# The next head's queries and keys placed before the second half of a head's attention blocks

## The chip, the cores and the metric

The kernel runs on one core of a Trainium2 chip. The metric is device time of one execution in microseconds (us), as the median of several runs. TensorE (PE) multiplies matrices, VectorE (DVE), ScalarE (ACT) and GpSimd (POOL) work element by element, and SyncE (SP) starts most transfers. Each engine takes its instructions strictly in the order in which the program lists them for it, and waits where an operand or a buffer isn't ready.

## The reference

Two residual layers with a pre-RMSNorm each, over 16 meta tokens and 1024 tokens of width 1024: a gated convolution layer, then a differential-attention layer with 8 heads, and a final RMSNorm. The change concerns the attention layer, which computes, in outline,

```
q, k, v, z = split(hn @ w_in)                       # per head: two q and two k of width 64, v of width 128
for i in range(9):                                  # blocks of 128 queries
    s = q_block @ k[:end].T * scale - slope * distance, masked
    p = softmax(s)
    a = p[first] - lam * p[second]
    o_block = a @ v[:end]
o = rms_norm(o, subln_gain) * (1 - lambda_init) * silu(z)
return o @ w_out
```

## The kernel before

Matrices are multiplied in float32r. A product with a weight is made of three passes (high part of the weight by high and by low part of the input, low part of the weight by the high part), so that one projected strip of 128 channels costs 24 matmuls per chunk of tokens. The input of the attention layer stays in SBUF for the whole layer.

For each head four things are made. `queries(h)` (L903) projects two chunks of 512 tokens into two PSUM banks of the pool "proj", which has two banks in all; DVE takes each chunk out with a scale (L910) into a tile "qt" of the pool "ev", which has two tiles; ACT and POOL split it (L915, and L157 through the helper). `keys(h)` (L921) does the same with three chunks of 348, 346 and 346 tokens (L925, L928, L157) and then copies the half tiles across partitions with four transfers on SP's queue (L934). `gate(h)` (L937) projects two chunks of 512, takes them into two "zt" tiles of the same pool "ev" (L944), and ACT makes their SiLU (L946), with a table load before and one behind it (L946, L948). The SiLU's result is the tile "za", of which there is one: it can't be written before the head before has read its own for the last time (L1055, in the last of its four block pairs). `attention(h, ...)` (L965) has four rounds j = 0 to 3, each of two blocks of 128 queries. Per block and per half m it makes scores in chunks of at most 512 columns (two matmuls each, L989 and L990) in a pool of three PSUM banks. DVE reduces them out of PSUM (L992), ACT exponentiates (L997), ACT and DVE normalise and combine (L1012, L1013), PE transposes (L1023, and L1034 for the last 16 columns), ACT and DVE take the transposes out in two parts (L1027, L1028). At the end of a round PE multiplies with the values (L207 into o, closed by the matmul of L1050), DVE multiplies with the gate (L1055), PE sums squares (L1063), ACT, POOL and DVE normalise, and SP stores the round to memory (ya_d, L1084). In the last head's time PE also begins the output projection (ao), for which SP reloads the stored rounds (L1132).

Nobody writes the engines' order by hand. The program is written head after head, and a scheduler with a timeline of its own picks, at each step, among the instructions that it takes for ready the one that stands first in the program; so the program's order is a priority. In the names of tiles, `s4_3_1_264` is head 4, block 3, half 1, first column 264; `q5_1` is head 5, chunk 1; `o3_3` is head 3, round 3; `tp` and `tc` are transposes. The call that the change rewrites is

```
ops = q2, *keys(0)
for h in range(HEADS):
    attention(h, *ops, sz)
    if h + 1 < HEADS:
        ops = queries(h + 1), *keys(h + 1)
        sz = gate(h + 1)
```

so that a head's queries, keys and gate stand behind the whole of the head before, and fill PE wherever attention isn't ready.

Of the kernel before, what the change touches and what calls it, by code (L numbers as in the profile page):

```python
# [28 lines left out]
HEADS = 8  # L29
# [66 lines left out]
def trunk(  # L96
# [25 lines left out]
    def stage(n, name, dt=F32):  # L122
        return gp.tile([P, T], dt, tag=f"st{n % 2}", name=name, bufs=1)

    def proj(name):
        return psg.tile([P, 512], F32, tag="proj", name=name, bufs=2)
# [29 lines left out]
    def lo_part(eng, out_, full, hi):  # L156
        return eng.tensor_tensor(out=out_, in0=full, in1=hi, op=ALU.subtract)  # L157
# [87 lines left out]
    def project(w, hh, hl, bank, chunks, release=False):  # L245

        wh, wl = w
        if release:
            os = [bank(ci) for ci in range(len(chunks))]
            for k in range(KD):  # L250
                for o, (c0, n) in zip(os, chunks):
                    cs = slice(c0, c0 + n)
                    passes(
                        o[:, :n], [wh[:, k]], [wl[:, k]], [hh[k][:, cs]], [hl[k][:, cs]],
                        start=k == 0, stop=k == KD - 1,
                    )
            for o, (c0, n) in zip(os, chunks):
                yield c0, n, o[:, :n]
            return
        for ci, (c0, n) in enumerate(chunks):  # L260
            o = bank(ci)
            passes(
                o[:, :n],
                [wh[:, k] for k in range(KD)],
                [wl[:, k] for k in range(KD)],
                [hh[k][:, c0 : c0 + n] for k in range(KD)],
                [hl[k][:, c0 : c0 + n] for k in range(KD)],
            )
            yield c0, n, o[:, :n]
# [473 lines left out]
    with ExitStack() as st1:  # L743
# [4 lines left out]
        def qk(name, shape=(P, T), dt=F32R):  # L748
            return sb.tile(list(shape), dt, tag="qk", name=name, bufs=12)
# [4 lines left out]
        def ev(name):  # L754
            return sb.tile([P, 512], F32, tag="ev", name=name, bufs=2)
# [148 lines left out]
        def queries(h):  # L904
            qs = -(2.0 ** (h + 1)) / math.sqrt(HD)
            q2 = [qk(f"q{m}_{h}", (P, SEQ)) for m in range(2)]
            for c0, w, o in project(weights.get(), hh, hl, lambda ci: proj(f"q{h}_{ci}"), RQ):
                cs = slice(c0 - META, c0 - META + w)
                t = ev(f"qt{h}_{c0}")[:, :w]
                V.scalar_tensor_tensor(  # L910
                    out=t, in0=o, scalar=qs, in1=rst[:, c0 : c0 + w], op0=ALU.mult, op1=ALU.mult
                )
                for m in range(2):
                    ms, other = slice(64 * m, 64 * m + 64), slice(64 - 64 * m, 128 - 64 * m)
                    A.activation(out=q2[m][ms, cs], in_=t[ms], func=AF.Copy)  # L915
                    lo_part(G, q2[m][other, cs], t[ms], q2[m][ms, cs].bitcast(F32))
            return q2

        def keys(h):
            k2 = [qk(f"k{m}_{h}") for m in range(2)]  # L920
            kl2 = [qk(f"kl{m}_{h}") for m in range(2)]  # L921
            for c0, w, o in project(weights.get(), hh, hl, lambda ci: proj(f"k{h}_{ci}"), CH):
                cs = slice(c0, c0 + w)
                t = ev(f"kt{h}_{c0}")[:, :w]
                V.tensor_tensor(out=t, in0=o, in1=rst[:, cs], op=ALU.mult)  # L925
                for m in range(2):
                    ms = slice(64 * m, 64 * m + 64)
                    A.activation(out=k2[m][ms, cs], in_=t[ms], func=AF.Copy)  # L928
                    lo_part(V if KL == "V" else G, kl2[m][ms, cs], t[ms], k2[m][ms, cs].bitcast(F32))

            for m in range(2):
                ms, other = slice(64 * m, 64 * m + 64), slice(64 - 64 * m, 128 - 64 * m)
                for t in (k2[m], kl2[m]):
                    SP.dma_start(out=t[other].bitcast(F32), in_=t[ms].bitcast(F32))  # L934
            return k2, kl2

        def gate(h):  # L937
            s = stage(1, f"za{h}")
            for c0, w, o in project(weights.get(), hh, hl, lambda ci: proj(f"za{h}_{ci}"), RQ, h in GREL):
                t = ev(f"zt{h}_{c0}")  # L940
                if h == 0:
                    A.activation(out=t, in_=o, func=AF.Copy)
                    o = t
                V.tensor_tensor(out=t, in0=o, in1=rst[:, c0 : c0 + w], op=ALU.mult)  # L944
                with tc.issue_after(last_exp) if h == 0 else ExitStack():
                    silu = A.activation(out=s[:, c0 - META : c0 - META + w], in_=t, func=AF.Silu).ins  # L946
            with tc.issue_after(silu):
                A.preload_act_table_set("natural_log_exp_and_others")  # L948
            return s
# [14 lines left out]
        def attention(h, q2, k2, kl2, sz):  # L964
# [6 lines left out]
            for j in range(4):  # L971
# [111 lines left out]
                if h < HEADS - 1:  # L1083
                    SP.dma_start(out=ya_d[h, :, :, js], in_=y2.bitcast(F32))  # L1084
                elif j > 1:
                    y_last.append([yh, yl])

        sz = gate(0)
        wv = [value_weights(0)]
# [3 lines left out]
            values(half, *wv[half])  # L1093
        ops = q2, *keys(0)
        for h in range(HEADS):
            attention(h, *ops, sz)
            if h + 1 < HEADS:
                ops = queries(h + 1), *keys(h + 1)
                sz = gate(h + 1)


        def strip_pair(make):
# [176 lines left out]
def _program(arrays):  # L1279
    import concourse.bacc as bacc  # L1280

    nc = bacc.Bacc("TRN2", target_bir_lowering=False, num_devices=1, dynamic_dma_scratch_size=8192)
    args = [
        nc.dram_tensor(n, a.shape, mybir.dt.from_np(a.dtype), kind="ExternalInput").ap() for n, a in arrays.items()
    ]
    args.append(nc.dram_tensor("out", (KD, P, SEQ), F32, kind="ExternalOutput").ap())
    with tile.TileContext(nc, schedule_with_timeline_sim=TLS) as tc:
        trunk(tc, *args)
    return nc
# [9 lines left out]
```

## Time and profile before

| | |
|---|---|
| time, median of 3 runs | 1468.54 us (1467.7 to 1470.9) |
| the profiled execution | 1467.64 us |
| its span, first to last instruction | 1465.5 us |
| mean granted TensorE clock | 0.991 of full speed |
| PE busy | 1423.4 us, 97% |
| DVE, ACT, POOL busy | 1115.3, 887.3, 811.7 us |

A busy PE includes the modelled tail of each matmul, so that a row of one instruction is longer than the distance to the next one. "x12" joins twelve instructions in sequence. Square brackets at the end of a row give the engine's idle time ahead of it, and what ended that. SPq is SP's queue.

### The profile page before, as it was taken

The numbers are of one execution on the slowest core, as the hardware profiler recorded it, in microseconds if no ns is written. First come the engines' busy times: TensorE is split into PE (matmuls) and PEld (weight loads), VectorE is DVE, ScalarE is ACT, GpSimd is POOL, SyncE is SP. The second block draws the span as 40 slices with busy tenths as digits, with TensorE's granted clock in tenths as the row PEclk, the third lists the DMA queues.
The fourth block names the chain that finished last, engine by engine and source line by source line (L and its number), as shares of the span: only waits on it lengthen the run. The fifth ranks groups of instructions, "written<-read, shape, count | busy, mean of one in ns | idle before, by whom it ended". The sixth has DMA issues, their size and how long they took to land.

```text
span 1465.5 us, 24123 instructions
## 1 busy us (share of the span) xinstructions
PE 1423.4 (97%) x8828; PEld 1333.3 (91%) x8828; DVE 1115.3 (76%) x2100; ACT 887.3 (61%) x1615; POOL 811.7 (55%) x646
## 2 busy tenths in 40 slices
PE   8999999999999999999999999999999999999997
PEld 7999999999999999899999878988889899897786
DVE  7989899899899988979545311578788787786774
ACT  7565665565555658766324411568778777786652
POOL 4598999999999940035014500525345354353572
PEclk9999999999999999999999999999999999999998
DMA  5021112112211333554443634223221322338532
GB/s 182 30 73 44 58 52 66 44 44 67 64 44 44 102 108 95 190 166 147 165 167 124 204 99 125 59 73 106 84 81 62 114 80 77 109 88 296 166 121 95
DMA packets 79928, 150.82 MB, mean 103 GB/s; under 512 B 6977, under 2 KB 46402, under 8 KB 78786
## 3 DMA queue, kind: packets, MB, share of 16 engines
q1 hardware_dynamic: 66706, 126.69, 27.3%
q0 software_dynamic: 3824, 13.37, 2.8%
q10 hardware_dynamic: 9280, 9.23, 2.0%
q8 instruction: 69, 1.13, 0.3%
q14 instruction: 49, 0.40, 0.1%
HBM read 106.73 MB, written 34.01 MB: 96 GB/s over the span
## 4 chain that ended last, share of the span: by engine, by line
PE 47%; POOL 18%; DVE 14%; ACT 8%; issue 8%; DMA 4%; SPq 1%; POOLq 0%; DVEq 0%; ACTq 0%
POOL pb L511 16%; PE c L207 8%; PE v L207 6%; PE k L207 5%; PE q L207 4%; PE za L207 4%; PE ao L207 3%; PE o L207 3%; PE u L207 3%; PE z L207 2%; DVE wl L157 2%; PE s L989 2%; ACT pr L510 2%; PE s L990 2%; PE tp L1023 2%
## 5 line engine op out<-in xcount | busy, mean ns | idle before, releaser
L511 POOL TENSOR_TENSOR pb<-pr,pb 128x521 f32<-128x521 f32 (+1 forms) x272 | 389.2, 1440 | 24.9 <-ACT pr L510 10.4
L510 ACT ACTIVATE pr<-vr,chn 128x521 f32<-128x521 f32 x224 | 150.6, 725 | 122.5 <-POOL pb L511 122.1
L207 PE MATMUL c<-b,wh 128*128 128x260 f32 x1024 | 187.3, 285 | 3.0 <-DVE b L157 1.9
L524 DVE SCALAR_TENSOR_TENSOR ev<-vr,chn,ev 128x520 f32<-128x520 f32 x240 | 181.2, 755 | 1.2
L189 ACT ACTIVATE wh<-wf 128x1024 fp32r<-128x1024 f32 x115 | 121.0, 1053 | 99.6 <-PE c L207 54.0
L207 PEld LDWEIGHTS c<-b,wh 128*128 128x128 f32 x1024 | 159.7, 191 | 3.8 <-DVE b L157 2.1
L207 PE MATMUL g<-hp,wh 128*128 128x346 f32 (+1 forms) x752 | 151.8, 329 | 7.6 <-ACT hp L383 3.6
L207 PE MATMUL u<-hp,wh 128*128 128x346 f32 (+1 forms) x752 | 155.9, 321 | 2.0 <-ACT wh L189 2.0
L207 PE MATMUL c<-b,wl 128*128 128x260 f32 x512 | 145.4, 286 | 3.8 <-DVE wl L157 3.8
L157 DVE TENSOR_TENSOR wl<-wf,wh 128x1024 fp32r<-128x1024 f32 x81 | 118.4, 1463 | 30.3 <-ACT wh L189 29.5
L157 POOL TENSOR_TENSOR wl<-wf,wh 128x1024 fp32r<-128x1024 f32 x34 | 85.7, 2521 | 92.9 <-ACT wh L189 47.4
L207 PEld LDWEIGHTS g<-hp,wh 128*128 128x128 f32 x752 | 127.6, 193 | 9.5 <-ACT hp L383 3.9
L207 PE MATMUL z<-hp,wh 128*128 128x346 f32 (+1 forms) x768 | 135.6, 321 | 0.5 <-ACT sig L469 0.5
L524 DVE SCALAR_TENSOR_TENSOR od<-xs,wc,od 128x520 f32<-128x520 f32 x176 | 132.6, 754 | 0.0
L696 POOL TENSOR_TENSOR total<-hsq,total 128x520 f32<-128x520 f32 x12 | 20.6, 1714 | 196.2 <-ACT hsq L695 196.2
L207 PEld LDWEIGHTS u<-hp,wh 128*128 128x128 f32 x752 | 125.7, 188 | 2.8 <-ACT wh L189 2.8
L207 PEld LDWEIGHTS z<-hp,wh 128*128 128x128 f32 x768 | 124.3, 188 | 0.9 <-ACT sig L469 0.7
L997 ACT ACTIVATE p<-p,st 128x272 f32<-128x272 f32 (+7 forms) x128 | 100.5, 785 | 39.3 <-DVE st L992 38.8
L207 PEld LDWEIGHTS c<-b,wl 128*128 128x128 f32 x512 | 97.7, 191 | 4.6 <-DVE wl L157 4.4
L207 PE MATMUL g<-hp,wl 128*128 128x346 f32 (+1 forms) x376 | 84.2, 322 | 0.0
L207 PE MATMUL v<-wv,g 128*128 128x512 f32 x352 | 83.5, 394 | 0.0
L989 PE MATMUL s<-k,q 128*128 128x256 f32 (+6 forms) x224 | 77.2, 349 | 5.3 <-DVE st L992 5.3
(292 smaller groups left out, 3465.1 us busy)
## 6 DMA issues: line engine op xcount, KB each, us to landing
wf<-conv_in SPq DMA_DIRECT2D x48, 512.0 KB, 3.5
wf<-conv_out SPq DMA_DIRECT2D x32, 512.0 KB, 4.1
wf<-attn_in SPq DMA_DIRECT2D x32, 512.0 KB, 3.8
wf<-attn_out SPq DMA_DIRECT2D x17, 512.0 KB, 3.7
sz_d<-sz ACTq DMA_DIRECT2D x32, 260.0 KB, 4.4
szr<-sz_d SPq DMA_DIRECT2D x16, 520.0 KB, 4.4
v<-v_d POOLq DMA_DIRECT2D x8, 1024.0 KB, 5.3
ya_d<-yb SPq DMA_DIRECT2D x28, 256.0 KB, 2.5
```

Source lines behind the costliest of these rows:

```text
L157: return eng.tensor_tensor(out=out_, in0=full, in1=hi, op=ALU.subtract)
L189: A.activation(out=wh, in_=wf, func=AF.Copy)
L207: PE.matmul(o, a[k], b[k], start=start and i == 0, stop=stop and i == tot - 1)
L510: A.activation(out=d, in_=src, func=AF.Copy, scale=w)
L511: G.tensor_tensor(out=dst, in0=d, in1=dst, op=ALU.add)
L524: V.scalar_tensor_tensor(out=dst, in0=src, scalar=w, in1=dst, op0=ALU.mult, op1=ALU.add)
L696: (V if SQA[m] == "V" else G).tensor_tensor(out=total[:, ns], in0=sq, in1=total[:, ns], op=ALU.add)
L989: PE.matmul(o[:, :wm], q2[m][:, qs], k2[m][:, c0 : c0 + wm], start=True, stop=False)
L990: PE.matmul(o[:, :wm], q2[m][:, qs], kl2[m][:, c0 : c0 + wm], start=False, stop=True)
L997: A.activation(out=p[:, :n], in_=p[:, :n], func=AF.Exp, scale=-1.0, bias=least, accum_out=st[:, 1:2],)
L1023: PE.transpose(tp[:, (kb - kb0) * P : (kb - kb0 + 1) * P], p0[:, kb * P : (kb + 1) * P], ident)
```

## The change

`attention` becomes a generator that yields at the end of each round. Behind round j = 1 the loop makes the next head's queries and keys; the gate is made where it was.

```
...
                elif j > 1:
                    y_last.append([yh, yl])
+                yield j
...
         for h in range(HEADS):
-            attention(h, *ops, sz)
+            for j in attention(h, *ops, sz):
+
+                if j == 1 and h + 1 < HEADS:
+                    coming = queries(h + 1), *keys(h + 1)
             if h + 1 < HEADS:
-                ops = queries(h + 1), *keys(h + 1)
-                sz = gate(h + 1)
+                ops, sz = coming, gate(h + 1)
```

No instruction is added or taken out. The strips of weights are still taken in the order queries, keys, gate. The scheduler then lists the instructions of the attention layer in another order on all engines. Three places follow. (The last number of a name is that of the buffer.)

On PE, in head 4, the stretch behind the end of `o3_3` up to the first matmul of the next head's keys, `k5_0`. Before:

```order
L1034 MATMUL tc4_1_12090<-ident_65,p4_1_0_12066 16x128
L207 MATMUL q5_1_12534<-g3_7604,wl95_11975 128x512
L1023 MATMUL tp4_2_0_12144<-ident_65,p4_2_0_12124 128x128 x4
L207 MATMUL q5_1_12534<-g4_7726,wl95_11975 128x512
L989 MATMUL s4_4_0_0_12229<-k0_4_11864,q0_4_11794 128x328
L990 MATMUL s4_4_0_0_12229<-kl0_4_11866,q0_4_11794 128x328
L989 MATMUL s4_4_0_328_12233<-k0_4_11864,q0_4_11794 128x328
L990 MATMUL s4_4_0_328_12233<-kl0_4_11866,q0_4_11794 128x328
L207 MATMUL q5_1_12534<-g5_7849,wl95_11975 128x512
L207 MATMUL q5_1_12534<-g6_7971,wl95_11975 128x512
L207 MATMUL q5_1_12534<-g7_8094,wl95_11975 128x512
L207 MATMUL k5_0_12575<-g0_7238,wh96_12499 128x348
```

With the change:

```order
L989 MATMUL s4_4_0_0_12406<-k0_4_11592,q0_4_11522 128x328
L990 MATMUL s4_4_0_0_12406<-kl0_4_11594,q0_4_11522 128x328
L1034 MATMUL tc4_1_12090<-ident_65,p4_1_0_12066 16x128
L989 MATMUL s4_4_0_328_12410<-k0_4_11592,q0_4_11522 128x328
L990 MATMUL s4_4_0_328_12410<-kl0_4_11594,q0_4_11522 128x328
L1023 MATMUL tp4_2_0_12144<-ident_65,p4_2_0_12124 128x128 x4
L1063 MATMUL o3_3_11926<-osq3_3_11952,ones_63 128x256
L989 MATMUL s4_4_1_0_12418<-k1_4_11593,q1_4_11523 128x328
L990 MATMUL s4_4_1_0_12418<-kl1_4_11595,q1_4_11523 128x328
L989 MATMUL s4_4_1_328_12422<-k1_4_11593,q1_4_11523 128x328
L990 MATMUL s4_4_1_328_12422<-kl1_4_11595,q1_4_11523 128x328
L207 MATMUL k5_0_12303<-g0_7238,wh96_12227 128x348
```

Before, matmuls of the queries `q5_1` stand between the scores, and the last of them directly ahead of `k5_0`; now they are all further up, and `k5_0` follows the scores of block 4.

On PE, in head 2, the stretch from the scores of block 2 to those of block 3. Before (the scores `s2_3_0_264` follow fifteen rows below the last one):

```order
L989 MATMUL s2_2_1_0_10732<-k1_2_10463,q1_2_10393 128x400
L990 MATMUL s2_2_1_0_10732<-kl1_2_10465,q1_2_10393 128x400
L207 MATMUL q3_0_11101<-g2_7481,wl89_10573 128x512
L207 MATMUL q3_0_11101<-g3_7604,wl89_10573 128x512
L1023 MATMUL tp1_7_1_10335<-ident_65,p1_7_0_10293 128x128 x4
L207 MATMUL q3_0_11101<-g4_7726,wl89_10573 128x512
L207 MATMUL q3_0_11101<-g5_7849,wl89_10573 128x512
L207 MATMUL q3_0_11101<-g6_7971,wl89_10573 128x512
L207 MATMUL q3_0_11101<-g7_8094,wl89_10573 128x512
L989 MATMUL s2_3_0_0_10751<-k0_2_10462,q0_2_10392 128x264
L990 MATMUL s2_3_0_0_10751<-kl0_2_10464,q0_2_10392 128x264
L207 MATMUL q3_1_11132<-g0_7238,wh89_10572 128x512
```

With the change:

```order
L989 MATMUL s2_2_0_0_10724<-k0_2_10190,q0_2_10120 128x400
L990 MATMUL s2_2_0_0_10724<-kl0_2_10192,q0_2_10120 128x400
L989 MATMUL s2_2_1_0_10732<-k1_2_10191,q1_2_10121 128x400
L990 MATMUL s2_2_1_0_10732<-kl1_2_10193,q1_2_10121 128x400
L989 MATMUL s2_3_0_0_10751<-k0_2_10190,q0_2_10120 128x264
L990 MATMUL s2_3_0_0_10751<-kl0_2_10192,q0_2_10120 128x264
L207 MATMUL o1_3_10524<-ath1_3_0_10424,v1_9932 128x256
L989 MATMUL s2_3_0_264_10755<-k0_2_10190,q0_2_10120 128x264
L990 MATMUL s2_3_0_264_10755<-kl0_2_10192,q0_2_10120 128x264
L1034 MATMUL tc1_7_10519<-ident_65,p1_7_0_10470 16x128
```

Before, matmuls of `q3_0` and `q3_1` stand between the score chunks; now the four chunks follow each other, with one matmul of `o1_3` among them.

On SP, the transfers around the first store of head 6 (`yb6_0`), the copies of head 7's keys, and the reloads (`a0` to `a5`). Before:

```order
L1084 DMA ya_d_8300<-yb6_0_13520 256x1x256
L1132 DMA a0_0_14595<-ya_d_8300 128x2x512
L1132 DMA a1_0_14596<-ya_d_8300 128x2x512
L934 DMA k0_7_13967<-k0_7_13967 64x1040
L934 DMA k1_7_13968<-k1_7_13968 64x1040
L1132 DMA a2_0_14597<-ya_d_8300 128x2x512
L934 DMA kl0_7_13969<-kl0_7_13969 64x1040
L934 DMA kl1_7_13970<-kl1_7_13970 64x1040
L173 DMA wf106_14659<-attn_out 128x1024
L1132 DMA a3_0_14598<-ya_d_8300 128x2x512
L1132 DMA a4_0_14599<-ya_d_8300 128x2x512
L1132 DMA a5_0_14600<-ya_d_8300 128x2x512
```

With the change:

```order
L934 DMA k0_7_13695<-k0_7_13695 64x1040
L1084 DMA ya_d_8300<-yb5_3_13369 256x1x256
L934 DMA k1_7_13696<-k1_7_13696 64x1040
L173 DMA wf106_14659<-attn_out 128x1024
L934 DMA kl0_7_13697<-kl0_7_13697 64x1040
L934 DMA kl1_7_13698<-kl1_7_13698 64x1040
L1084 DMA ya_d_8300<-yb6_0_13520 256x1x256
L1135 DMA a0_0_14595<-ya_d_8300 128x2x512
L1135 DMA a1_0_14596<-ya_d_8300 128x2x512
L1135 DMA a2_0_14597<-ya_d_8300 128x2x512
L1198 DMA f0_14601<-h1_d_78 128x1024 x2
L1135 DMA a3_0_14598<-ya_d_8300 128x2x512
L1135 DMA a4_0_14599<-ya_d_8300 128x2x512
```

Before, the copies of head 7's keys stand among the reloads; now they stand ahead of the store of `yb6_0`, and the two loads of `f0` stand ahead of `a3`.

## Rows read from the trace of the kernel before

**Rows 1.** The page: the span, and the granted clock in 40 slices.

```profile
span 1465.5 us, 24123 instructions
...
PEclk9999999999999999999999999999999999999998
```

**Rows 2.** Busy time by stretch: the attention heads (engine busy, count; clock last but two).

```profile
909.00:1400.00 491.00, 479.91 (x2810) 428.99 (x2808) 365.30 (x1020) 364.76 (x775) 228.17 (x226) 1.00 0.35 109
```

**Rows 3.** PE's waits, 900 to 1400 us: total, times, longest.

```profile
PE s L989 <- DVE st L992: 5.3, 4, 1.8
PE ao L207 <- DMA a<-ya_d: 1.7, 3, 0.8
PE k L207 <- DVE qt L910: 1.2, 2, 0.9
PE s L990 <- DMA kl<-kl: 1.2, 2, 0.6
```

**Rows 4.** Timeline of PE, head 1: start, duration, instruction, idle before it.

```profile
989.36 0.39 PE L989 MATMUL s<-k,q 128*128 128x264 f32 x1 [1.76 <-DVE st L992]
...
993.30 0.28 PE L1050 MATMUL o<-cor,vm 80*128 80x256 f32 x1
...
995.05 0.70 PE L1063 MATMUL o<-osq,ones 128*128 128x256 f32 x2
995.46 0.44 PE L989 MATMUL s<-k,q 128*128 128x328 f32 x1
...
998.10 1.06 PE L207 MATMUL k<-g,wh 128*128 128x348 f32 x5 [0.92 <-DVE qt L910]
```

**Rows 5.** Timeline of ACT, the same stretch.

```profile
995.40 1.28 ACT L946 ACT_TABLE_LOAD   x1
996.69 1.15 ACT L946 ACTIVATE za<-zt 128x512 f32<-128x512 f32 x2
999.15 0.74 ACT L997 ACTIVATE p<-p,st 128x528 f32<-128x528 f32 x1
```

**Rows 6.** Timeline of DVE, heads 1, 2, 4 and 6: the queries taken out of PSUM.

```profile
997.36 1.29 DVE L910 SCALAR_TENSOR_TENSOR qt<-q,hsum 128x512 f32<-128x512 f32 x2 [0.48 <-ACT za L946]
...
1054.68 1.29 DVE L910 SCALAR_TENSOR_TENSOR qt<-q,hsum 128x512 f32<-128x512 f32 x2 [0.27 <-ACT za L946]
...
1164.58 0.69 DVE L910 SCALAR_TENSOR_TENSOR qt<-q,hsum 128x512 f32<-128x512 f32 x1 [0.83 <-ACT za L946]
...
1281.00 0.69 DVE L910 SCALAR_TENSOR_TENSOR qt<-q,hsum 128x512 f32<-128x512 f32 x1 [0.49 <-ACT za L946]
```

**Rows 7.** Timeline of PE, heads 2, 4 and 6.

```profile
1051.24 0.28 PE L1050 MATMUL o<-cor,vm 80*128 80x256 f32 x1
...
1055.42 0.74 PE L207 MATMUL k<-g,wh 128*128 128x348 f32 x3 [0.32 <-DVE qt L910]
...
1160.96 0.28 PE L1050 MATMUL o<-cor,vm 80*128 80x256 f32 x1
...
1163.42 2.95 PE L207 MATMUL q<-g,wh 128*128 128x512 f32 x12
...
1277.51 0.28 PE L1050 MATMUL o<-cor,vm 80*128 80x256 f32 x1
```

**Rows 8.** Timeline of SP's queue around the reloads.

```profile
1311.31 1.20 SPq L934 DMA_DIRECT2D k<-k  x2
...
1313.61 2.21 SPq L934 DMA_DIRECT2D kl<-kl  x2
...
1316.83 2.62 SPq L1132 DMA_DIRECT2D a<-ya_d  x3
...
1322.72 1.03 SPq L1195 DMA_DIRECT2D f<-h_d  x2
```

**Rows 9.** Busy time by stretch: head 1's waits, and the reloads.

```profile
984.00:999.00 15.00, 12.13 (x78) 10.19 (x77) 12.57 (x34) 11.30 (x25) 5.63 (x8) 1.00 0.38 124
1321.00:1335.00 14.00, 11.11 (x47) 8.33 (x46) 7.71 (x25) 6.42 (x19) 3.46 (x3) 0.88 0.98 337
```

## The prediction

> **What bounds the kernel now.** I read the page first, then the busy time by stretch, then PE's waits, and last the timelines at the places of those waits. The page shows a span of 1465.5 us and full granted clock nearly throughout [rows 1]. Over the attention heads, 909 to 1400 us, PE is busy for 479.9 of 491 us, DVE for 365 and ACT for 365 [rows 2]: PE sets the time, and the change takes no work from it. All that an order can win there is PE's visible idle time, 491 − 479.9 = 11.1 us; what it can lose has no such limit. Four kinds of wait make up 9.4 us of it [rows 3]: scores that wait for a bank that DVE must empty (5.3), output strips that wait for reloads (1.7), keys that wait for a bank that DVE must empty of queries (1.2), scores that wait for the copies of the keys (1.2).
>
> The wait on which I build is the third. In head 1 the round o0_3 ends on PE with the matmul at 993.30; the first matmul of the next keys, k2_0, begins at 998.10 and has waited 0.92 us for "DVE qt" [rows 4]. k2_0 needs the bank of q2_0. DVE can empty that only into a "qt" tile, both tiles of that pool hold the gate's "zt", and these come free through the gate's SiLU, which must wait until o0_3 has been multiplied with the old gate. On ACT this shows as a table load at 995.40 (1.28 us) and two SiLUs (1.15 us) [rows 5]; DVE's eviction starts at 997.36, after an idle time that ACT's "za" ended, and the first of its two instructions ends 0.69 us later, at 998.05 [rows 6]. So **the keys of the head after next can't start earlier than some 4 us behind a head's last round, whatever their priority**: 998.05 − 993.58 = 4.5 us in head 1, and by the same two rows 3.9 in head 2, 4.0 in head 4, 3.9 in head 6 [rows 6, 7]. The mean is 4.1 us.
>
> **The change part by part.** Nothing is added or removed. Seven times the queries (per head 48 matmuls, 2 evictions on DVE, 4 splits on ACT, 4 on POOL), the keys (72 matmuls, 3, 6 and 6) with four copies on SP, and the preparation of their weights on SP, ACT and POOL get priority over the second half of a head's blocks. DVE and ACT have about 126 us free in the stage [rows 2], POOL over 260: their share costs nothing by itself, and only a wait of PE does.
>
> *Term 1, the keys' bank.* The order shows what fills PE between a head's last round and k_0. In head 4 it was 24 matmuls of q5 and a few scores; now it is scores and transposes alone, since q5 has been used up earlier. Twelve matmuls of 512 columns take 2.95 us with the modelled tail of the last one [rows 7], 0.23 us apiece without it. Ten score matmuls with 3152 columns in all are then 1.45 us, five transposes 0.4, the sum of squares 0.4 (995.05 to 995.46 [rows 4]): 2.3 us, where the 24 query matmuls alone were 5.6. Counted alike for the other heads, the cover is 1.8, 2.4, 4.7, 2.3, 3.4 and 2.3 us in heads 1 to 6; before it was 2.4 and 3.4 in heads 1 and 2, and over 7 in the four others, which is why rows 3 has only two such waits. With 4.1 us needed, PE will lack 2.3 + 1.7 + 0 + 1.8 + 0.7 + 1.8 = 8.3 us, against (4.5 − 2.4) + (3.9 − 3.4) = 2.6 now: **+5.7 us**. Behind k_0 in PE's queue stand the scores of block 4 or 5, so DVE and ACT wait with it. Bounds: if only table load, half of the SiLUs and one eviction lay on the path (1.28 + 0.58 + 0.69 = 2.6 us [rows 5, 6]), 1.2 us would be lacking in all, which is −1.4 against now; in heads 4 and 6 the new order also puts an exponential of 528 columns (0.74 us [rows 5]) ahead of the table load, and with 4.5 us for all it becomes +9. I take 5.7, from the rows of the same chain.
>
> *A rule on the table load.* The row of the table load is 1.28 us long, and the SiLU behind it starts 0.01 us after its end [rows 5]. The Trainium skill, "ScalarE: Activation LUTs", section "What ACT_TABLE_LOAD costs", adds about 1.38 us of drain to a load, 2.66 us per switch; no idle time before the SiLU shows this here. By that rule term 1 would be some +11 us; the measured chains already hold what the load costs, so I keep the rows.
>
> *Term 2, scores without filler.* In head 2 the four score chunks of blocks 2 and 3 now follow each other, with one matmul between the second bank and its reuse, where twenty query matmuls stood. Heads 4 and 6 look alike. The nearest row is head 1 of before, which had this shape and lost 1.76 us there [rows 4]. In head 1 itself the round o0_3 now stands ahead of that score, and its wait should go. Between 0 and 3 × 1.8 come, 1.8 go: −1.8 to +3.6, and I take the middle, **+1.0**.
>
> *Term 3, the last head.* The copies of head 7's keys are issued ahead of the first store of head 6 and no longer among the reloads: the 1.2 us that scores wait for them go [rows 3], **−1.2**. The reloads a3 to a5 lose 1.2 + 2.2 us of key copies ahead of them in the queue and gain 1.0 us of loads of f0 [rows 8], which themselves wait for the last gate's matmuls; and the store in front of them comes later, since the sums of o6_0 stand some 7 us of PE's work further down. Either way PE's 1.7 us of waits there [rows 3] move by no more than a few us, and with them a stretch at a lower clock (0.88 over 14 us, 1.7 us lost [rows 9]). Bounds −3.4 and +4; I take **0**.
>
> Sum: 5.7 + 1.0 − 1.2 + 0 = +5.5 us on the profiled execution's 1467.64 us (2.1 us of it lie outside the span): 1473.1. The median shown is 0.9 us higher than that execution, so I predict **1474.0 us**.
>
> **Rivals.** (A) *The waits only change places.* PE, DVE and ACT have the same work, and what PE waits for at k_0 it may save at a later score, since DVE and ACT catch up meanwhile; the 5.3 us for scores [rows 3] give room for that. Against it: those waits sit in heads 1, 5 and 7, not behind k_0. About 1468.5 us, within 2 of it.
> (B) *Faster, through the last head.* The key copies and the reloads no longer wait for each other: −1.2, −1.7 for the reloads, −1.7 for the clock behind them, and −1.8 for head 1's score, while the chain behind the gate runs at its bare 2.6 us and term 1 is −1.4. It decides at a chain of about 2.9 us: above, the keys' waits eat the gain. With half of term 1 still standing: some 1464 us. For it: all these waits are in rows 3 and 4; against it: none of the four measured chains is below 3.9.
> (C) *The clock falls too.* In 1321 to 1335 us a cluster of waits (PE busy 11.1 of 14 us) came with a granted clock of 0.88, while in 984 to 999 us waits of like size (12.1 of 15) left it at 1.00 [rows 9]. If each of the five new waits brought the lower level (1.2 instead of 2.4 GHz) for as long as there, 5 × 1.7 = 8.4 us come on top: 1482. The Trainium skill, "TensorE: Matmul & The Clock Gate", section "A second HAM failure mode: psum-queue depth-cycling", says that a kernel that idles briefly at each change of PSUM banks can swing between the two levels; by that rule (C) would be the forecast. Head 1's row, with just such a wait for a bank at full clock, speaks against it, so it stays a rival.
>
> **How the numbers follow.** About 0.2%, 2.9 us, is what a measurement here can tell from no change. Forecast (+3 to +10 us) 0.48; (C) 0.12; (A) 0.22; (B) 0.18. Slower by over 0.2%: 0.48 + 0.12 = 0.60; same 0.22; faster 0.18. The likeliest case's own range is 1471.5 to 1479. The range for 8 in 10 reaches down to (B)'s 1464 and up to 1482 for the upper bounds of the terms and (C).
>
> **What would show it.** Right: in PE's waits of the changed kernel, "k <- DVE qt" grows from 1.2 us in 2 places to 4 us or more in four or five, one per head, with ACT's SiLU as DVE's own releaser; "s <- DMA kl" is gone; PE's busy time outside is unchanged. Wrong: if "k <- DVE qt" stays near 1 us, the chain behind the last round is shorter than 4 us or its cover was larger than I counted, and term 1 falls; if the time goes into scores waiting for DVE, term 2 was the larger; if the granted clock drops in the middle heads, (C) holds.

## The result and the profile after

| | before | after |
|---|---|---|
| median | 1467.57 us (1465.95 to 1470.9, 6 runs) | 1475.87 us (1473.81 to 1477.93, 6 runs) |
| ratio of the times, 95% interval | 1 | 1.0054 [1.0044, 1.0065] |
| span of the profiled execution | 1465.5 us | 1474.9 us |

The change makes the kernel slower by 0.54%, 7.9 us. Forecast were 1474.0 us and "slower". The rows of the changed kernel follow in the order of those of before. First the page and, in a second fence, the busy time of the attention heads:

```profile
span 1474.9 us, 24106 instructions
...
PEclk9999999999999999999999999999999999999998
```

```profile
909.00:1400.00 491.00, 476.23 (x2763) 425.58 (x2761) 364.54 (x1016) 360.06 (x765) 218.86 (x221) 0.99 0.34 107
```

PE's visible idle time in these 491 us has grown from 11.1 [rows 2] to 14.8 us, and less work was done in them: PE has 47 instructions fewer. Where the idle time stands, PE's waits tell, first those up to 1400 us, then those behind:

```profile
PE k L207 <- DVE qt L910: 5.2, 4, 1.6
PE s L989 <- DVE st L992: 5.1, 5, 1.8
PE ao L207 <- DMA a<-ya_d: 2.0, 1, 2.0
...
PE ft L1180 <- POOL fsq L1172: 2.2, 1, 2.2
PE ao L207 <- DVE yb L157: 1.6, 1, 1.6
```

Against [rows 3]: the keys' wait for the queries' bank rose from 1.2 us in two places to 5.2 in four, the scores' wait for the keys' copies (1.2 us) is gone, the reloads are much the same, and the scores' wait for DVE looks the same (5.3, now 5.1). It isn't the same, as will be seen. The last line but one is new: before, that wait for POOL was 0.4 us.

The chain behind a head's last round, in head 4, first on PE, then on ACT, then on DVE:

```profile
1172.39 0.36 PE L1050 MATMUL o<-cor,vm 80*128 80x256 f32 x1
...
1175.61 0.31 PE L990 MATMUL s<-kl,q 128*128 128x328 f32 x1
1177.56 1.70 PE L207 MATMUL k<-g,wh 128*128 128x348 f32 x9 [1.64 <-DVE qt L910]
```

```profile
1174.03 0.72 ACT L997 ACTIVATE p<-p,st 128x528 f32<-128x528 f32 x1
1174.65 0.18 ACT L997 ACTIVATION_READ_ACCUMULATOR p<-p,st 128x1 f32 x1
1174.86 1.28 ACT L946 ACT_TABLE_LOAD   x1
1176.15 1.15 ACT L946 ACTIVATE za<-zt 128x512 f32<-128x512 f32 x2
```

```profile
1174.00 0.47 DVE L1055 SCALAR_TENSOR_TENSOR ya<-o,sub_s,za 128x256 f32<-128x256 f32 x1
...
1176.81 0.69 DVE L910 SCALAR_TENSOR_TENSOR qt<-q,hsum 128x512 f32<-128x512 f32 x1 [1.00 <-ACT za L946]
```

The round ends on PE at 1172.75, DVE multiplies with the old gate, ACT loads the table and makes SiLU, DVE's eviction waits 1.00 us for "za", and 0.06 us behind the eviction's end the keys begin: 4.8 us after the round. The table load doesn't begin when the multiplication ends (1174.47) but when ACT has done an exponential of 528 columns (1174.83). The wait of the keys was not there before the change [rows 6, 7]: PE had 24 query matmuls in it.

### The profile page after: what moved, and what is told of

The parts are those of the page before. It is cut to its first block, busy times and chain, and to the rows that moved or that the text cites. A ratio compares the mean times of both kernels' runs of the same rounds, so it can differ in the third digit from the quotient of the medians.

```text
span 1474.9 us, 24106 instructions
## 1 busy us (share of the span) xinstructions
PE 1427.8 (97%) x8828; PEld 1336.5 (91%) x8828; DVE 1117.1 (76%) x2100; ACT 888.2 (60%) x1615; POOL 806.8 (55%) x646
## 4 chain that ended last, share of the span: by engine, by line
PE 54%; POOL 17%; DVE 13%; ACT 7%; issue 7%; DMA 2%; POOLq 0%; DVEq 0%; ACTq 0%; SPq 0%
POOL pb L511 16%; PE c L207 12%; PE k L207 6%; PE v L207 6%; PE za L207 5%; PE q L207 5%; PE ao L207 4%; PE u L207 3%; PE o L207 3%; PE z L207 2%; PE s L989 2%; PE s L990 2%; ACT pr L510 2%; PE tp L1023 2%; PE g L207 2%
```

## What was to be told apart

Theory P is the prediction's: the keys are pinned behind the gate's SiLU, since DVE's evictions of the queries need the tiles that hold "zt", and with the queries used up earlier PE has too little to do until then. Theory S: the loss comes from scores that follow each other without filler (term 2). Theory K: clock, last head and tail. A fourth, H, came out of the traces after the first four runs: DVE is held by POOL.

## The experiments

**The queries in a tile of their own,** in the changed kernel and in the one before:

```
-                t = ev(f"qt{h}_{c0}")[:, :w]
+              for p0 in (0, 256):
+                t = sb.tile([P, 256], F32, tag="qx", name=f"qt{h}_{c0}_{p0}", bufs=1)
...
```

(The edit also takes out `ones_r`, a constant that this kernel never reads, with the one ACT instruction that fills it.)

> The changed kernel, but the queries leave PSUM through a tile of their own (1 KB, four takes of 256 columns a head in place of two of 512), so that the gate's SiLU no longer stands between a head's last round and the next keys. Theory P (the keys are pinned behind the gate's SiLU by the shared pool): the waits k <- qt, 5.2 us in the changed kernel, fall below 1 us, and the time falls from 1475.9 us by 4 to 8 us, to 1468 to 1472. Theory S (the loss is that scores follow each other without filler; the keys' waits are only where it shows): k <- qt falls, s <- st rises from 5.1 us to about 10, and the time stays within 2 us of 1475.9. Theory K (the loss lies in the clock and in the last head's and the tail's waits): the time stays above 1474, with granted clock below full in the middle heads or a wait of some 2 us in the tail.

> The kernel before with the same edit (the queries in a tile of their own). It is the control for the edit itself. Theory P: only the 1.2 us of k <- qt in 2 places can go, so 1466 to 1468 us, at most 2 us below 1467.6. If it falls by 4 us or more, the own tile gives something else than theory P says, and the fall of the changed kernel with the edit is no proof. Theories S and K expect no change, 1467.6 within 2.

Measured: the changed kernel 1472.12 us, ratio 1.0020 [1.0008, 1.0033]; the kernel before 1461.41 us, 0.9948 [0.9936, 0.9961]. The first fell by 0.34%, 5 us, as P says; but the control fell by 0.52%, 7.6 us, where P allowed 2, and the distance between the two kernels went from 7.9 to 10.6 us. So P alone doesn't carry it. PE's waits to 1400 us with the edit, in the changed kernel and in the kernel before (an edit moves line numbers by a few):

```profile
PE af L207 <- ACT y L1080: 3.4, 1, 3.4
PE k L207 <- DVE kt L926: 1.8, 3, 1.0
...
PE o L1062 <- DVE ya L1054: 1.3, 2, 0.7
PE tp L1022 <- DVE p L1012: 1.2, 1, 1.2
```

```profile
PE k L207 <- DVE kt L926: 1.7, 1, 1.7
...
PE s L988 <- DVE st L991: 0.5, 2, 0.3
PE k L207 <- DVE qt L911: 0.3, 1, 0.3
```

"k <- qt" is gone in the changed kernel, as P wants. The pin is not gone, it has moved: the keys still leave PSUM through the pool that holds "zt". In five heads DVE's eviction of their first chunk waits for the SiLU, 4.9 us in all, and PE's keys wait behind it for a bank ("k <- kt", 1.8 us). DVE, in head 1:

```profile
1004.09 0.52 DVE L926 TENSOR_TENSOR kt<-k,hsum 128x348 f32<-128x348 f32 x1 [0.72 <-ACT za L947]
```

A version in which the keys too have tiles of their own was not run. In the kernel before, the waits for "st" are nearly gone too (5.3 to 0.5 us), which P doesn't connect with the queries' tile, and the changed kernel has waits in new places: for "ya", for "p", for "y". Behind one of those, at 1070 us of the changed kernel with the edit, stand these instructions of DVE and of POOL:

```profile
1068.93 2.60 DVE L1072 SCALAR_TENSOR_TENSOR ya<-ox,ya 128x256 f32<-128x256 f32 x1 [1.64 <-POOL ya L1066]
1071.46 0.47 DVE L1054 SCALAR_TENSOR_TENSOR ya<-o,sub_s,za 128x256 f32<-128x256 f32 x1
```

```profile
1068.86 2.40 POOL L157 TENSOR_TENSOR wl<-wf,wh 128x1024 fp32r<-128x1024 f32 x1
```

A DVE instruction of 256 columns took 2.60 us, where the one behind it, of the same kind and size but with an input in PSUM, took 0.47. POOL had begun 0.07 us ahead of it with the subtraction that makes the low part of a weight strip, and DVE ended 0.27 us after POOL. The same pattern stands behind the 1.76 us for which the scores of block 3 in head 2 wait in the changed kernel (DVE, POOL, PE):

```profile
1045.89 2.07 DVE L1013 SCALAR_TENSOR_TENSOR p<-p,st,p 128x272 f32<-128x272 f32 x1
1048.10 0.57 DVE L992 CUSTOM_DVE_ANT_0 p<-s,total 128x400 f32<-128x400 f32 x1
```

```profile
1045.28 2.38 POOL L157 TENSOR_TENSOR wl<-wf,wh 128x1024 fp32r<-128x1024 f32 x1 [10.32 <-PE q L207]
```

```profile
1048.73 0.39 PE L989 MATMUL s<-k,q 128*128 128x264 f32 x1 [1.76 <-DVE st L992]
```

In the kernel before, head 1's wait of 1.76 us [rows 4] has it as well (DVE, POOL):

```profile
985.95 2.63 DVE L1013 SCALAR_TENSOR_TENSOR p<-p,st,p 128x272 f32<-128x272 f32 x1
```

```profile
985.92 2.36 POOL L157 TENSOR_TENSOR wl<-wf,wh 128x1024 fp32r<-128x1024 f32 x1 [10.21 <-PE q L207]
```

That wait was my nearest row for "scores without filler"; it was DVE held by POOL. The Trainium skill, "SBUF — State Buffer", section "Who interferes with whom", states that a DVE instruction with two inputs in SBUF and a GpSimd instruction that reads SBUF exclude each other for a whole instruction; the rows agree.

**The queries alone early, and both a round later:**

```
-                    coming = queries(h + 1), *keys(h + 1)
+                    coming = queries(h + 1)
...
-                ops, sz = coming, gate(h + 1)
+                ops = coming, *keys(h + 1)
+                sz = gate(h + 1)
```

> Only the queries precede the second half of a head's blocks; the keys stay at the end of the head, ahead of the gate. By the order, PE's cover between a head's last round and the next keys is 2.4, 3.1, 5.9, 6.5, 8.3, 8.3 us in heads 1 to 6. Theory P: with 4.1 us needed, 1.7 + 1.0 = 2.7 us are lacking, k <- qt 1 to 3 us, the time 1467 to 1470. Theory S (the queries, used up early, are missing as filler among the scores): the time stays at 1474 or above, with s <- st above 7 us.

> Queries and keys one round later, ahead of the last quarter of a head's blocks. By the order, the cover is 2.4, 5.0, 3.7, 2.7, 4.6, 4.8 us in heads 1 to 6. Theory P: 1.7 + 0 + 0.4 + 1.4 + 0 + 0 = 3.5 us lacking, k <- qt 3 to 4 us, the time 1470 to 1473. Theory S: more filler is left for the scores of blocks 4 to 7, s <- st below 5 us and the time within 2 us of 1467.6 whatever the keys' waits. Theory K: no forecast beyond 1467 to 1476.

(For the second the edit is `if j == 2` in place of `if j == 1`.) Measured: 1462.83 us, 0.9958 [0.9946, 0.9969], and 1467.49 us, 0.9988 [0.9975, 1.0]. "k <- qt" was 1.5 us in 2 places and 2.9 in 4, in the order that the covers asked for (2.7 and 3.5); "s <- st" was 2.1 and 2.3 us. The second came out below P's 1470 and as S had it, so it decides nothing. S falls with the first: early queries made the scores' waits no longer. It is the early keys that cost, 14 us between the first kernel here and the changed one (0.9958 to 1.0054). That the first beats the kernel before by 6 us, and stays 4 us below P's range, P doesn't explain: two waits of 1.7 us for "st", in heads 5 and 7, didn't happen in it.

**POOL's subtraction cut in four,** in both kernels, alone and with the queries' tile:

```
-            lo_part(eng, wl, wf, wh.bitcast(F32))
+                for k in range(0, KD, 2):
+                    lo_part(eng, wl[:, k : k + 2], wf[:, k : k + 2], wh.bitcast(F32)[:, k : k + 2])
```

> The changed kernel, with POOL's subtraction for each strip of the attention layer's weights (1024 columns, 2.4 us in the trace) cut into four of 256 columns. Theory H (the scores' waits are not for want of filler: a DVE instruction with two inputs in SBUF is held until POOL's long subtraction ends, as at 1045.89 us, where one of 272 columns took 2.07 us, median 0.50): s <- st falls from 5.1 us to below 2, the time by 3 to 6 us, to 1470 to 1473; k <- qt stays at 3 to 6 us. Theory S (scores without filler): s <- st stays above 4 us, the time within 2 us of 1475.9. A price of cutting, four fixed costs in place of one on POOL, lies off the path on either theory.

> The kernel before with the same cut of POOL's subtractions. Theory H: its three waits of 1.7 us for DVE behind such a subtraction (heads 1, 5 and 7) go, s <- st from 5.3 us to below 2, the time falls by 3 to 5 us, to 1463 to 1465; the distance between the changed kernel and this one stays at 6 to 9 us, since both had about 5 us of these waits. Theory S: no change, 1467.6 within 2.

> The changed kernel with both edits, the queries in a tile of their own and POOL's subtractions cut. Theories P and H together: neither k <- qt nor the 1.7 us waits for st are left, and with DVE's holds away the distance to the kernel before with both edits falls from 10 us to within 3: 1461 to 1466 us. If the pin is not what the change costs, the distance stays at 6 us or more, and this kernel at 1467 or above.

> The kernel before with both edits. Theory H: little is left to win, since the one edit already took s <- st from 5.3 to 0.5 us: 1459 to 1462, against 1461.4 with the queries' tile alone. It is the yardstick for the changed kernel with both edits.

Measured, as ratios to the kernel before, with the distance between the two kernels in us (intervals of 1.5 us either way without an edit, about 2.6 with one):

| edit | kernel before | changed kernel | distance, by the ratios |
|---|---|---|---|
| none | 1 | 1.0054 | 7.9 |
| queries' tile | 0.9948 | 1.0020 | 10.6 |
| POOL cut | 0.9929 [0.9916, 0.9942], 1459.0 us | 1.0008 [0.9996, 1.0020], 1469.93 us | 11.6 |
| both | 0.9938 [0.9924, 0.9952], 1460.41 us | 0.9954 [0.9942, 0.9966], 1462.35 us | 2.3 |

PE's waits to 1400 us, with the cut alone in the changed kernel, then in the kernel before, and with both edits in the changed kernel:

```profile
PE s L994 <- DVE st L997: 2.7, 8, 0.5
PE k L211 <- DVE qt L915: 2.4, 3, 1.3
```

```profile
PE k L211 <- DVE qt L915: 0.9, 1, 0.9
...
PE s L994 <- DVE st L997: 0.4, 1, 0.4
```

```profile
PE s L993 <- DVE st L996: 0.9, 3, 0.5
...
PE k L211 <- DVE kt L931: 0.4, 1, 0.4
```

H holds: the longest wait for "st" fell from 1.8 to 0.5 us and from 1.8 to 0.4, and both kernels gained. Its sizes were off. In the changed kernel "s <- st" kept 2.7 us (below 2 expected) and "k <- qt" fell to 2.4 (3 to 6 expected); the kernel before gained 10 us where 3 to 5 stood, of which the waits for "st" make up 4.9; the distance grew to 11.6 us where 6 to 9 stood. Only with both edits does it fall to 2.3 us, which the interval doesn't tell from nothing. In this version "k <- qt" is absent and "k <- kt" is 0.4 us. This is what P asks for, and the strongest sign that the pin makes up most of what the change costs. It is no measure of it: with each edit the scheduler orders all engines anew, each version is one such order, and an order can win or lose some us by other means (the queries' tile won 7.6 us in the kernel before, where P allowed 2). Each edit alone left 11 us and both together 2, so the two do not add; that a hold and a pinned bank make each other's delay visible is a reading of this, not shown by a row. How the 11.6 us with the cut alone divide isn't settled by the waits: "k <- qt" differs by 1.5 us, "s <- st" by 2.3, and the profiled spans by 16.5, of which each execution's scatter is part.

**More pin, and the pin by heads,** all with POOL's subtraction cut:

> POOL's subtractions cut, and the gate too is made behind round 1, so that queries, keys and gate all precede the second half of a head's blocks. By the order, PE's cover between a head's last round and the keys after next is 2.9, 1.8, 2.4, 2.1, 1.8, 2.4 us in heads 1 to 6: with 4.1 us needed, 11.2 us are lacking, against 5.8 in the changed kernel with POOL's subtractions cut alone. Theory P: k <- qt rises from 2.4 to 5 us or more, in five or six places, and the time from 1469.9 by 4 to 8 us, to 1474 to 1478. If the keys' pin is not what costs (only the order of DVE's work, or the last head), the time stays at 1468 to 1472.

> POOL's subtractions cut, and the change made in heads 0 to 2 alone; heads 3 to 6 as in the kernel before. By the order, the cover is 1.8, 2.4, 4.7, 6.6, 8.6, 8.5 us: 4.0 us lacking, all of it in heads 1 and 2, against 3.3 in the kernel before with the cut alone (1459.0 us) and 5.8 in the changed one (1469.9). Theory P: k <- qt 1 to 3 us, the time 1459 to 1463. If the change costs the same in each head, 3/7 of 11 us: 1464.

> POOL's subtractions cut, and the change made in heads 3 to 6 alone. By the order, the cover is 2.4, 2.7, 6.7, 2.3, 3.4, 2.3 us: 7.4 us lacking, more than in the changed kernel with the cut (5.8). Theory P: k <- qt 3 to 6 us, three of them in heads 4 to 6, the time 1466 to 1472. If the change costs the same in each head, 4/7 of 11 us: 1465; if its cost lies in heads 0 to 2, 1460.

> POOL's subtractions cut, and the queries alone behind round 1: the best half of the change with the cut. The cover is 2.4, 2.7, 6.7, 5.9, 3.9, 7.6 us, as in the kernel before with the cut (1459.0 us), 3.3 us lacking. Theories P and H: 1456 to 1461, level with that kernel; the 6 us by which the queries alone beat the kernel before without the cut (1462.8 against 1469.5) came from where POOL's long subtractions fell, and are not won twice. If early queries are a gain of their own: 1453 to 1455.

The edits are `coming = queries(h + 1), *keys(h + 1)` with `sz2 = gate(h + 1)` behind it, `if j == (1 if h < 3 else 3)`, `if j == (1 if h >= 3 else 3)`, and the queries alone as above. Measured: 1511.55 us, 1.0297 [1.0283, 1.0312]; 1460.70 us, 0.9958 [0.9945, 0.9971]; 1465.66 us, 0.9986 [0.9976, 0.9996]; 1461.62 us, 0.9960 [0.9947, 0.9973].

The two halves cost 4.3 and 8.4 us against the kernel before with the cut (0.9929), together 12.7 where the whole change costs 11.6. The times alone don't decide between P and "the same in each head" (the second half came out at 1465.7, a little under P's 1466 to 1472); for the second half the waits do. From 1100 to 1300 us, heads 3 to 6, PE has no wait at all for queries or scores where the change was made in heads 0 to 2. Where it was made in heads 3 to 6 it has:

```profile
PE k L211 <- DVE qt L915: 3.5, 3, 1.7
PE s L994 <- DVE st L997: 1.1, 3, 0.6
```

They stand in heads 4, 5 and 6, with 1.64, 0.19 and 1.66 us where the covers lacked 1.8, 0.7 and 1.8. The first half's 4.3 us (2.7 either way) are not in such waits: its "k <- qt" is 1.3 us in one place, the kernel before with the cut has 0.9.

The early gate shows something else. Its "k <- qt" rose to 5.2 us in six places, as P said, but the kernel lost 42 us, not 4 to 8:

```profile
PE tp L1028 <- DVE p L1018: 8.3, 7, 2.9
PE s L994 <- DVE st L997: 5.5, 11, 1.4
PE tp L1028 <- DVE st L1006: 5.4, 4, 2.4
PE k L211 <- DVE qt L915: 5.2, 6, 1.4
```

The transposes of a head's last blocks wait for the softmax (13.7 us in 11 places). The likely reading is that with queries, keys and gate all ahead of the second half nothing is left to fill PE at a head's end, and that the change stays within 8 us because it leaves the gate there. PE's waits show about half of the loss: up to 1400 us they add up to 29.9 us, against 9.0 in the changed kernel with the cut.

The queries alone with the cut, 1461.62 us, don't beat the kernel before with the cut: the 6 us that they won without it are not won twice, as expected. By the ratios they are even 4.5 us slower (2.7 either way), just above the expected range, with the same 0.9 us of "k <- qt". So some of the cost of a new order is not in the keys' waits, here and in the first half above, and stays open. The best version is the kernel before with POOL's subtraction cut, 1459.0 us, 0.71% under the kernel before.

## Why the prediction was right

**The bound and term 1.** PE sets the time, and the new wait stands where the prediction put it, for the reason that it gave: in head 4 every link of the chain can be read, and it lasts 4.8 us (4.4 in head 1; 4.1 was taken). Measured were 5.2 − 1.2 = +4.0 us in "k <- qt", forecast +5.7. By heads: 1.33 us in head 1 (2.3 forecast), 1.64 in head 4 (1.8), 0.62 in head 5 (0.7), 1.64 in head 6 (1.8), none in head 2 (1.7). That heads 4 to 6 agree so well is partly luck, because both parts of the difference were taken too small. From the end of the round to the keys it took 4.4, 4.1, 4.8, 4.4 and 6.2 us in heads 1, 2, 4, 5 and 6, where 4.1 was taken for all. PE's cover, from the end of the round to the start of the wait, was 3.1, 4.0, 3.2, 3.7 and 4.6 us, where 1.8, 2.4, 2.3, 3.4 and 2.3 had been counted: the count took every column at the pace of the query matmuls, and waits between were not in it. Head 6 is the largest case. A score waited 1.35 us for DVE inside the chain, and the first matmul of a score took 0.23 us to the next one (1294.04 to 1294.27), where the count has 0.15 for 328 columns:

```profile
1289.65 0.36 PE L1050 MATMUL o<-cor,vm 80*128 80x256 f32 x1
1291.37 0.39 PE L989 MATMUL s<-k,q 128*128 128x264 f32 x1 [1.35 <-DVE st L992]
...
1294.04 0.40 PE L989 MATMUL s<-k,q 128*128 128x328 f32 x1
1294.27 0.31 PE L990 MATMUL s<-kl,q 128*128 128x328 f32 x1
1296.22 1.06 PE L207 MATMUL k<-g,wh 128*128 128x348 f32 x5 [1.64 <-DVE qt L910]
```

Term 1 as a size is 1.7 us too large in this view; as a cause it stands, the largest wait that the change adds. Its lower bound was added up wrong: with a chain of 2.6 us the covers lack 0.8 + 0.2 + 0.3 + 0.3 = 1.6 us, not 1.2, which makes it −1.0 and (B) 0.4 us slower.

**The rule on the table load.** The SiLU starts 0.01 us after the load's end again (1176.15 against 1174.86 + 1.28). The +11 us estimated from the Trainium skill's "ScalarE: Activation LUTs", section "What ACT_TABLE_LOAD costs", for term 1 are not in the waits, and keeping the rows was right.

**Term 2 is the step that failed.** "Scores without filler", +1.0 us, took head 1's wait as its row. The total came out at −0.2 us, inside its bounds, but by other means: new waits in head 2 (1.76 us), head 4 (0.84) and head 6 (1.35), two of 1.7 us gone in heads 5 and 7, and head 1's, which was to go, down from 1.76 to 0.93. All of these depend on which DVE instruction POOL's subtraction catches. A trace row that names "DVE st" as the releaser says only who came last; what made DVE late stood in the length of the DVE instruction ahead (2.63 us for 272 columns), and I didn't read that.

**Term 3** held: the copies' wait went (−1.2 us), and the reloads moved by +0.3 us (0 forecast).

**What the sum left out.** Busy time from the first matmul of head 0's keys to the end, before and after (stretch, length, PE):

```profile
909.74:1465.50 555.76, 533.17 (x3211) 479.23 (x3209) 406.57 (x1081) 387.66 (x819) 257.11 (x250) 0.99 0.35 108
```

```profile
908.11:1474.90 566.79, 538.12 (x3211) 483.73 (x3209) 407.73 (x1081) 388.09 (x819) 251.68 (x250) 0.98 0.34 106
```

The stretch grew by 11.0 us (ahead of it, in work that the change doesn't touch, after was 1.6 us quicker), and PE's visible idle time in it from 22.6 to 28.7 us, +6.1. Of these 1.8 are the tail's wait for POOL, which stands behind three multiplications of 5.15 us together:

```profile
1432.47 5.15 POOL L1191 TENSOR_TENSOR f<-f,fr 128x512 f32<-128x512 f32 x3
1437.58 1.17 POOL L1172 TENSOR_TENSOR fsq<-fsq 128x256 f32<-128x256 f32 x1
```

It was 1.6 to 3.6 us in eleven of the twelve experiments above, the kernels before with an edit among them, and absent in the twelfth (the changed kernel with the queries' tile); so it isn't tied to this change, and the 0.4 us of the kernel before is an exception. Then the clock. Busy time in three short stretches of the changed kernel: two that ran slow, and the keys' wait in head 4 (clock last but two):

```profile
1167.70:1170.90 3.20, 3.20 (x17) 3.20 (x16) 3.00 (x11) 1.96 (x6) 0.52 (x1) 0.50 0.27 108
...
1440.70:1443.90 3.20, 3.20 (x16) 3.09 (x14) 0.42 (x1) 0.00 (x0) 0.00 (x0) 0.50 0.12 47
1175.00:1180.00 5.00, 3.36 (x21) 3.01 (x20) 3.94 (x14) 4.96 (x8) 0.00 (x0) 1.00 0.47 179
```

In this part of the span PE ran at 0.50, its level of 1.2 GHz, twice more than before, for some 3.4 us and 1.7 us lost each time (ahead of it, once less): after two waits in a row in head 4 (0.55 and 0.84 us ahead of 1167), where DVE was held once more (1.56 us for an instruction with a median of 0.50), and after the tail's wait. The keys' waits themselves left the clock at 1.00 in this execution (in heads 1 and 6 too). That is no rule: in the changed kernel with the cut, behind a wait of 1.34 us for the keys' bank in head 1, where the changed kernel's 1.33 us left it at 1.00, the clock fell:

```profile
999.90:1003.10 3.20, 3.20 (x13) 3.20 (x12) 2.29 (x7) 3.16 (x7) 0.65 (x2) 0.50 0.22 70
```

The length of a wait thus doesn't tell whether the lower level follows, and one execution doesn't tell how often: over six executions the changed kernel's mean granted clock was 0.988 to 0.993. So rival (C) was right that the clock is part of it; in the execution shown it was wrong in where and how often. The remainder of the +11.0, 11.0 − 6.1 − 3.4 = 1.5 us, lies in no wait that the trace shows, and stays open.

**The rivals.** (A) fell: waits changed places only among those that POOL makes. (B) needed a chain below 2.9 us; the shortest, in head 3, where it is covered, is 3.6.

That the total came within 2 us is thus partly luck: term 1 was taken 1.7 us too large and term 2 too large by 1.2, and in the execution shown 5.2 us of clock and tail weren't in the sum.

## What to carry to other kernels

When work is moved ahead, ask which buffer its results leave PSUM through, and who holds that buffer until when: priority can't move an instruction ahead of a chain on three other engines, and it takes away the work that hid the chain. What stands at the end of a stage is filler; leave there what nobody needs soon, and move forward only what does not wait for the stage's last result. Before calling a wait "for DVE", compare the DVE instruction ahead of it with its like; one that is several times too long was held, and POOL's rows at that moment say by what.

## What the runs showed of the hardware that I had not expected

A subtraction of 1024 columns on POOL (2.4 us) held a DVE instruction with two inputs in SBUF that began 0.03 to 0.6 us behind it until 0.3 us after its own end: 2.63, 2.60 and 2.07 us for work of some 0.5 us. DVE instructions with an input in PSUM kept their length: of the subtractions at L1028 with 512 columns, twelve of the kernel before began during one of POOL's, and the longest took 0.69 us, where the median of the others is 0.68. Of the DVE instructions of the attention layer with both inputs in SBUF, thirteen began there, and all ended 0.17 to 0.57 us behind POOL's subtraction, the wider ones later. Cutting the subtraction in four cost POOL more time (its busy time over the attention layer and the tail rose from 257.1 to 272.8 us in the kernel before), and with it came 10 us, the largest gain of the study: making the work of an engine with time to spare slower. Half of that gain is in the scores' waits for DVE (4.9 us); for the other half no run shows that the holds are its cause.
